# Decoder trunk on one core: in 24 of 80 groups of products the columns are walked in another order

## The chip, the cores and the metric

The kernel runs on one core of one Trainium2 chip. The metric is the device time in microseconds (us) of one execution; the median of three runs is quoted. A profile of one execution, taken by the hardware, gives the rows that are read below. TensorE is called PE in them, its loading of stationary operands PEld, VectorE DVE, ScalarE ACT, GpSimd POOL and SyncE SP.

## The reference

The program is a decoder trunk of two layers over 256 tokens with 2048 features, all in float32. Cut to what matters:

```python
for layer in range(2):
    h = rms_norm(x, norm_g[layer])
    proj = h @ w_in[layer]                                  # 256 x 2048 by 2048 x 14336
    q, k, v, g_att, glu_a, glu_b, g_conv = split(proj)      # 2048 columns each
    q, k = apply_rope(rms_norm(q)), apply_rope(rms_norm(k))
    att = dilated_mixture(q, k, v)                          # 16 heads of 128
    att_y = rms_norm(att, att_out_g[layer]) * silu(g_att)
    u = depthwise_conv31(glu_a * sigmoid(glu_b)) + dw_bias
    conv = silu(layer_norm(u)) @ w_pw[layer]                # 2048 x 2048
    conv_y = rms_norm(conv, conv_out_g[layer]) * silu(g_conv)
    x = x + concat(att_y, conv_y) @ w_out[layer]            # 4096 x 2048
```

## The kernel before

**The large products.** All weights are cut into groups: a group is 2048 rows by 512 columns of one matrix, and its result is 256 tokens by 512 columns, in two banks of PSUM, `ps[0]` and `ps[1]`, of 128 tokens by 512 columns each. A layer has 40 groups: for each quarter `j` of the features `glu_b`, `glu_a`, `v`, `q`, `k` (20 groups); then `g_conv` 0, `g_att` 0 to 3, `g_conv` 1 to 3; then four `o_att`, four `pw` and four `o_conv`. So there are 80 groups in two layers, and `g_att`, `g_conv` and `o_att` have eight each.

**Steps.** A group is eight steps. A step has one weight tile of two times 128 rows by 512 columns (512 KB), loaded by SP's queue into `raw` (L220). ScalarE rounds it to the float32r tile `whi` (L227), VectorE writes the remainder to `wlo` (L228). The stationary operand, 128 features by 128 tokens, has such a pair too, `sthi` and `stlo`. TensorE makes three products for each 128 rows and each half of the tokens:

```python
T.matmul(ps[tt], xh, hi[:, kk], start=(k == 0), stop=False)
T.matmul(ps[tt], xh, lo[:, kk], start=False, stop=False)
T.matmul(ps[tt], xl, hi[:, kk], start=False, stop=(k == KT - 1))
```

These are L629, L630 and L631: 12 in a step, 96 in a group, 7680 in all. In each the moving operand is 512 columns of float32r, read from SBUF in the order in which they lie, and the 512 sums are written and added to in the same order in one bank. Splits are put into the program three steps ahead.

**The rest of the work.** Everything else (rotary positions, attention, the depthwise convolution, norms, transposes) is made of tasks that are cut into slices. The class `Filler` puts a slice into the program behind a step where its estimate of each engine's progress says that it fits. It estimates a step at 2.6 us of TensorE. The order of every engine's instructions is thus fixed when the program is built.

**Who uses the sums.** When a group is done, a task empties its banks: `ev_g_att` (ScalarE, L507), `ev_g_conv` (ScalarE, L501), `ev_o_att` (VectorE, L517). There are four banks for the sums, so the next group fills two while the former two are emptied. These tasks read 512 columns in the order in which they lie.

Of the kernel before, what the change touches and what calls it, by code (L numbers as in the profile page):

```python
# [22 lines left out]
KT = D // 128  # L23
NCH = 4
CH = 512
EPS = 1e-6
# Columns of the per-feature parameters: the taps by layer, then pairs by layer.
P_BIAS, P_LNG, P_LNB, P_ATT, P_CONV = (DEPTH * CW + DEPTH * i for i in range(5))
NPRM = DEPTH * (CW + 5)

# Weight tiles of [128, KS, CH]: a step is the products of one of them.
KS = 2
NSTEP = KT // KS
R_RAW, R_SPLIT = 4, 4
AHEAD = 3


class Need:
    """What the next slice of a task takes: time by engine (us, in the order in which its operations follow
    from one another), PSUM banks, and a condition that has to hold first."""  # L40

    def __init__(self, banks=0, when=None, **time):
        self.banks, self.when, self.time = banks, when, list(time.items())
# [3 lines left out]


class Filler:
    """Work beside the large products, in slices between their steps.  # L50

    A task is a generator that yields the Need of its next slice. The engines work in program order, so a
    slice is put into the program where its operands will about have been computed, by an estimate of how
    far each engine has got, and not where it would make the splits of the next weight tiles late."""

    HOP = 0.2

# [29 lines left out]
            self.banks.append((b, self.now[4]))  # L87

    def use(self, time, ready):
        """The time at which operations that follow from one another end, the first not before ready."""  # L90
        start = end = ready
        for e, cost in time:
            start = max(self.t[e], start)
            end = max(start + cost, end + 0.3)
            self.t[e] = end
            if e == "G":  # shares VectorE's port
                self.t["V"] = max(self.t["V"], start) + cost
                end += 1.0
            start += 0.45
        return end + self.HOP  # L100
# [43 lines left out]
def trunk(ctx: ExitStack, tc: tile.TileContext, x, norm_g, w_in, q_norm_g, k_norm_g, dw_kernel, dw_bias,  # L144
# [6 lines left out]
    V, S, G, T = nc.vector, nc.scalar, nc.gpsimd, nc.tensor  # L151

    def t(shape, name, dt=F32):
        return sb.tile(shape, dt, name=name)

    # Stationary operands by chunk of four contraction tiles, as exact sums hi + lo of float32r.
    st_hi = [[t([128, 4, SEQ], f"sthi{s}{c}", F32R) for c in range(4)] for s in range(2)]
    st_lo = [[t([128, 4, SEQ], f"stlo{s}{c}", F32R) for c in range(4)] for s in range(2)]
    Y = [t([128, 4 * SEQ], f"y{c}") for c in range(4)]
    A = [t([128, 2, CH], f"a{c}") for c in range(4)]  # L160
# [35 lines left out]

    xs = [dr.tile([SEQ, CH], F32, name=f"xs{c}") for c in range(NCH)]

# [1 line left out]
    groups = []  # L200
    for l in range(DEPTH):
        for j in range(NCH):
# [7 lines left out]
    tiles = [(g, s) for g in range(len(groups)) for s in range(NSTEP)]  # L210
# [12 lines left out]
    def split(i):  # L223
        if i >= len(tiles):
            return
        a, hi = raw[i % R_RAW], whi[i % R_SPLIT]
        S.activation(hi, a, AF.Copy)  # L227
        V.tensor_sub(wlo[i % R_SPLIT], a, hi.bitcast(F32))  # L228
        halved[i] = fill.use([("A", 0.95), ("V", 1.14)], loaded[i])
        load(i + R_RAW)  # L230

# [1 line left out]
    ready = [[False] * 4 for _ in range(2)]  # a chunk of the operand is in place  # L233
    vacant = [[True] * 4 for _ in range(2)]  # all its products are in the program
    flags = set()

    def flag(*what):
# [2 lines left out]
    def has(*what):  # L240
        return lambda: what in flags

    def rsqrt(r, ss, scale, n):
        """r = (ss * scale + EPS) ** -0.5 on [128, n]"""
        G.tensor_scalar(r, ss, scale, EPS, op0=ALU.mult, op1=ALU.add)
        G.tensor_tensor(r, r, half[:, :n], op=ALU.pow)

    def transposes(src, banks):
        """[128 tokens, 2, 4 x 128] -> two banks of [128, 2, 256 tokens]"""
        for b in range(2):  # L250
            for i in range(2):
                for tt in range(2):
                    e = (2 * b + i) * 128
                    T.transpose(banks[b][:, i * SEQ + tt * 128:i * SEQ + tt * 128 + 128],  # L254
                                src[:, tt, e:e + 128], ident)

    def to_stationary(src, s, c, gain):
        """Transposes a chunk and splits it, times a gain per feature."""
        yield Need(2, lambda: vacant[s][c], P=0.9)
        banks = [fill.bank(), fill.bank()]  # L260
        transposes(src, banks)
        yield Need(A=1.5, V=1.6)
        p = [b[:, i * SEQ:(i + 1) * SEQ] for b in banks for i in range(2)]
        for i in range(4):
            S.activation(st_hi[s][c][:, i], p[i], AF.Copy, scale=gain(i))  # L265
        for i in range(4):
            V.scalar_tensor_tensor(st_lo[s][c][:, i], p[i], gain(i), st_hi[s][c][:, i].bitcast(F32),  # L267
                                   op0=ALU.mult, op1=ALU.subtract)
        fill.free(*banks)
        filled(s, c)  # L270

    def filled(s, c):
        vacant[s][c] = False
        ready[s][c] = True

    def x_chunk(l, c):
        """A chunk of the residual stream, in A, becomes the next layer's operand."""
        yield from to_stationary(A[c], 0, c, lambda i: ng[:, l * KT + 4 * c + i:l * KT + 4 * c + i + 1])
        fill.add(x_square(l, c), 3, fill.now[4])

    def x_square(l, c):
        yield Need(A=1.4)
        for tt in range(2):
            S.activation(junk, A[c][:, tt], AF.Square, accum_out=ssx[:, tt, c:c + 1])  # L284
        flag("x", l, c)
        if all(("x", l, k) in flags for k in range(4)):
            yield Need(V=0.1, G=0.6)
            V.tensor_reduce(rsc, ssx, axis=mybir.AxisListType.X, op=ALU.add)
            rsqrt(rx, rsc, 1.0 / D, 2)
            flag("rx", l)  # L290
# [58 lines left out]
    def ln_square(l, j):  # L349
# [23 lines left out]
        V.tensor_copy(rsc, ps[:, 0:4:2])  # L373
        fill.free(ps)
        rsqrt(rstd, rsc, 1.0 / D, 2)
        G.tensor_copy(rbc, rstd[:, :, None].to_broadcast([128, 2, 128]))
        yield Need(1, P=0.5)
# [165 lines left out]
            yield from x_chunk(l + 1, j)  # L543
            nc.sync.dma_start(xs[j].rearrange("(t p) e -> p t e", p=128), A[j])

# [1 line left out]
    ng_in = t2[:DEPTH * KT, :128]  # L547
    S.dma_start(ng_in, norm_g.rearrange("l (k p) -> (l k) p", p=128))
    make_identity(nc, ident)
# [6 lines left out]
    r = 0  # L556
# [45 lines left out]
    for c in range(NCH):  # L602
        fill.add(x_chunk(0, c), 0)
    fill.add(parameters(), 1, 45.0)
    split(0)

# [1 line left out]
    users = {"glu_b": ev_glu_b, "glu_a": ev_glu_a, "v": ev_v, "g_conv": ev_g_conv, "g_att": ev_g_att,  # L608
             "pw": ev_pw, "o_att": ev_o_att, "o_conv": ev_o_conv,
             "q": lambda l, j, ps: ev_qk(l, j, ps, "q"), "k": lambda l, j, ps: ev_qk(l, j, ps, "k")}  # L610
# [1 line left out]
    for i, (g, s) in enumerate(tiles):  # L612
        l, nm, j, _, _, _, st = groups[g]
        c = s * KS // 4
        fill.until(lambda: ready[st][c])
        if s == 0 and g >= 2:
            fill.until(has("ev", *groups[g - 2][:3]))
        for a in range(i + AHEAD if i else 1, i + AHEAD + 1):
            split(a)
        ps = [acc[(2 * g + tt) % 4] for tt in range(2)]  # L620
        hi, lo = whi[i % R_SPLIT], wlo[i % R_SPLIT]
        order = [(kk, tt) for kk in range(KS) for tt in range(2)]
        if s == NSTEP - 1:
            order.sort(key=lambda o: o[1])
        for kk, tt in order:
            k = s * KS + kk
            tok = slice(tt * 128, tt * 128 + 128)
            xh, xl = st_hi[st][c][:, k % 4, tok], st_lo[st][c][:, k % 4, tok]
            T.matmul(ps[tt], xh, hi[:, kk], start=(k == 0), stop=False)  # L629
            T.matmul(ps[tt], xh, lo[:, kk], start=False, stop=False)  # L630
            T.matmul(ps[tt], xl, hi[:, kk], start=False, stop=(k == KT - 1))  # L631
        fill.use([("P", 2.6)], halved[i])
        if i >= 2 and later:
            nc.sync.dma_start(*later.pop(0))
        if i == NSTEP:
            G.dma_start(mask, log_count)
            rope_tables(0)
        if s % 2 and j == NCH - 1 and nm in last[st]:
            ready[st][c], vacant[st][c] = False, True
        if s == NSTEP - 1:  # L640
            fill.add(users[nm](l, j, ps), 0, fill.t["P"])
            if nm == "o_att" and j == NCH - 1 and l + 1 < DEPTH:
                rope_tables(l + 1)
        fill.run()
# [8 lines left out]


def log_counts():
    """By query (in its tile of 128) and key: the log of how many branches attend it."""
    q = np.arange(SEQ)[:, None]
    k = np.arange(SEQ)[None, :]
    d = q - k
    count = np.zeros((SEQ, SEQ))  # L660
    for window, dil in ((128, 1), (512, 4), (2048, 16)):
        count += (d >= 0) & (d <= window) & (d % dil == 0)
    m = np.where(count > 0, np.log(np.maximum(count, 1)), -1e30).astype(np.float32)
    return np.ascontiguousarray(np.concatenate([m[:128, :128], m[128:]], 1))
# [23 lines left out]
```

## Time and profile before

| what | value |
|---|---|
| median of three runs | 1864.1 us |
| the three runs | 1864.1, 1865.67 and 1863.65 us |
| span of the profiled execution, first to last instruction | 1863.1 us |
| TensorE busy | 1849.6 us, 99% |
| VectorE busy | 1394.8 us, 75% |
| ScalarE busy | 988.8 us, 53% |
| moved by DMA | 349.98 MB, 188 GB/s over the span |

The page gives no time for the profiled execution other than its span; the runs' median lies 1.0 us above that. The duration of a matmul in the rows is from its start to its modelled end; consecutive ones overlap, so what one takes of the span is read from the distance between two starts, or from a count in a stretch. A large product has one record; a float32 product of the small kind (L451, L452 and the like) has two records for one instruction of the program, so that a row of 64 stands for 32 of them.

### The profile page before, as it was taken

How to read it: one execution, taken by the hardware profiler on the slowest of the kernel's cores; microseconds unless marked ns; L12 is line 12 of the kernel's file. 1: busy time of each engine (PE TensorE's matmuls, PEld its weight loads, DVE VectorE, ACT ScalarE, POOL GpSimd, SP SyncE). 2: the span in 40 equal slices, each digit the busy share in tenths (PEclk: the TensorE clock that was granted, in tenths of full speed). 3: DMA queues.
4: the chain of work that ended last, by engine and by line, in shares of the span. 5: the costliest groups of instructions: out<-in, count | busy, mean ns of one | idle time of the engine just before them, and what ended most of it. 6: DMA issues, size and time to landing. Idle time of an engine off the chain costs nothing.

```text
span 1863.1 us, 23820 instructions
## 1 busy us (share of the span) xinstructions
PE 1849.6 (99%) x8525; PEld 1541.2 (83%) x8525; DVE 1394.8 (75%) x2160; ACT 988.8 (53%) x1559; POOL 136.3 (7%) x153
## 2 busy tenths in 40 slices
PE   8999999999999999999999999999999999999999
PEld 6888888888888888888888888888888888888887
DVE  4778889888889885556558888797887998755554
ACT  5465564564654464445444655646556445644542
POOL 1110100100110140000000101002000102100000
PEclk9999999999999999999999999999999999999999
DMA  7765656656566676666666656566565666666564
GB/s 237 204 184 167 180 180 180 182 168 190 174 180 193 177 231 210 192 190 190 208 203 192 188 161 184 159 199 183 160 185 165 194 195 190 213 204 195 178 205 145
DMA packets 180880, 349.98 MB, mean 188 GB/s; under 512 B 11064, under 2 KB 11096, under 8 KB 180760
## 3 DMA queue, kind: packets, MB, share of 16 engines
q1 hardware_dynamic: 179176, 345.61, 61.2%
q0 software_dynamic: 960, 1.77, 0.5%
q8 instruction: 67, 1.10, 0.2%
q10 hardware_dynamic: 624, 1.07, 0.2%
q14 instruction: 53, 0.43, 0.1%
HBM read 344.21 MB, written 4.19 MB: 187 GB/s over the span
## 4 chain that ended last, share of the span: by engine, by line
PE 97%; DMA 2%; ACT 0%; SPq 0%; DVE 0%; issue 0%; ACTq 0%; DVEq 0%
PE acc L630 31%; PE acc L631 31%; PE acc L629 31%; PE ax L254 2%; DMA raw<-in_w_in 2%; PE ax L452 1%; PE ax L469 1%; PE ax L478 0%; PE ax L477 0%; PE ax L476 0%; PE ax L451 0%; ACT whi L227 0%; DVE wlo L228 0%; SPq L551 0%; ACT junk L284 0%
## 5 line engine op out<-in xcount | busy, mean ns | idle before, releaser
L228 DVE TENSOR_TENSOR wlo<-raw,whi 128x1024 fp32r<-128x1024 f32 x640 | 792.2, 1246 | 404.5 <-ACT whi L227 400.4
L227 ACT ACTIVATE whi<-raw 128x1024 fp32r<-128x1024 f32 x640 | 675.3, 1063 | 671.1 <-PE acc L631 471.5
L629 PE MATMUL acc<-whi,sthi 128*128 128x512 f32 x2560 | 1005.9, 393 | 2.7 <-ACT whi L227 2.7
L630 PE MATMUL acc<-wlo,sthi 128*128 128x512 f32 x2560 | 998.1, 390 | 0.8 <-DVE wlo L228 0.8
L631 PE MATMUL acc<-whi,stlo 128*128 128x512 f32 x2560 | 998.3, 390 | 0.0
L629 PEld LDWEIGHTS acc<-whi,sthi 128*128 128x128 f32 x2560 | 481.7, 188 | 100.9 <-ACT whi L227 3.1
L631 PEld LDWEIGHTS acc<-whi,stlo 128*128 128x128 f32 x2560 | 481.5, 188 | 101.0
L630 PEld LDWEIGHTS acc<-wlo,sthi 128*128 128x128 f32 x2560 | 481.8, 188 | 98.8 <-DVE wlo L228 1.1
L326 DVE SCALAR_TENSOR_TENSOR y<-ut,prm,y 128x256 f32<-128x256 f32 x960 | 411.1, 486 | 0.0
L414 POOL TENSOR_SCALAR qr<-qss 128x8 f32<-128x8 f32 x16 | 3.2, 197 | 692.1 <-ACT junk L411 692.1
L411 ACT ACTIVATE junk<-acc,rx 128x128 bf16<-128x128 f32 x128 | 47.1, 368 | 8.4 <-PE acc L631 4.8
L334 POOL TENSOR_TENSOR ysum<-ysum,y 128x256 f32<-128x256 f32 x30 | 31.8, 1058 | 237.1 <-DVE y L326 235.7
L421 ACT ACTIVATE d<-acc,qr 128x128 f32<-128x128 f32 x128 | 34.8, 383 | 18.0 <-POOL qr L416 18.0
L265 ACT ACTIVATE sthi<-ax,prm 128x256 fp32r<-128x256 f32 x64 | 25.1, 475 | 31.1 <-PE ax L254 31.1
L267 DVE SCALAR_TENSOR_TENSOR stlo<-ax,prm,sthi 128x256 fp32r<-128x256 f32 x64 | 26.5, 475 | 15.8 <-ACT sthi L265 15.8
L442 ACT ACTIVATE c<-ax 128x512 f32<-128x512 f32 x32 | 17.4, 597 | 33.6 <-PE ax L254 33.6
L465 ACT ACTIVATE sm<-sm,smm 128x128 f32<-128x128 f32 x64 | 28.2, 443 | 6.6 <-DVE smm L460 6.6
L362 POOL TENSOR_TENSOR ssum<-ssum,d 128x512 f32<-128x512 f32 x14 | 26.8, 1912 | 5.9 <-ACT d L355 5.0
L415 POOL TENSOR_TENSOR qr<-qr,half 128x8 f32<-128x8 f32 x16 | 26.3, 1642 | 1.3
L254 PEld LDWEIGHTS ax<-ident,d 128*128 128x128 f32 x192 | 22.4, 140 | 3.2
L254 PE MATMUL ax<-ident,d 128*128 128x128 f32 x192 | 24.9, 273 | 0.0
L411 ACT ACTIVATION_READ_ACCUMULATOR junk<-acc,rx 128x1 f32 x128 | 24.7, 193 | 0.0
(106 smaller groups left out, 669.4 us busy)
## 6 DMA issues: line engine op xcount, KB each, us to landing
raw<-in_w_in SPq DMA_DIRECT2D x448, 512.0 KB, 3.9
raw<-in_w_out SPq DMA_DIRECT2D x128, 512.0 KB, 4.6
raw<-in_w_pw SPq DMA_DIRECT2D x64, 512.0 KB, 4.6
a<-in_x SPq DMA_DIRECT2D x8, 512.0 KB, 5.7
xs<-a SPq DMA_DIRECT2D x4, 512.0 KB, 6.0
a<-xs SPq DMA_DIRECT2D x4, 512.0 KB, 6.5
out<-a SPq DMA_DIRECT2D x4, 256.0 KB
out<-a ACTq DMA_DIRECT2D x4, 256.0 KB, 5.1
```

Of the source, the lines that this page charges most:

```text
L227: S.activation(hi, a, AF.Copy)
L228: V.tensor_sub(wlo[i % R_SPLIT], a, hi.bitcast(F32))
L254: T.transpose(banks[b][:, i * SEQ + tt * 128:i * SEQ + tt * 128 + 128], src[:, tt, e:e + 128], ident)
L326: V.scalar_tensor_tensor(y[:, c], u[:, c, k:k + SEQ], w[:, c, l * CW + k:l * CW + k + 1], y[:, c], op0=ALU.mult, op1=ALU.add)
L334: G.tensor_add(ysum, ysum, y[:, c])
L362: G.tensor_add(ssum, ssum, half_sq)
L411: S.activation(junk[:, :DH], ps[tt][:, h * DH:(h + 1) * DH], AF.Square, scale=rx[:, tt:tt + 1], accum_out=qss[:, tt, h:h + 1])
L421: S.activation(n[:, tt, h * DH:(h + 1) * DH], ps[tt][:, h * DH:(h + 1) * DH], AF.Copy, scale=qr[:, tt, h:h + 1])
L465: S.activation(s[:, cs], s[:, cs], AF.Exp, bias=m[:, tt:tt + 1], scale=-1.0, accum_out=lsum[:, tt:tt + 1])
L629: T.matmul(ps[tt], xh, hi[:, kk], start=(k == 0), stop=False)
L630: T.matmul(ps[tt], xh, lo[:, kk], start=False, stop=False)
L631: T.matmul(ps[tt], xl, hi[:, kk], start=False, stop=(k == KT - 1))
```

## The change

In the groups of three names the moving operand and the sums are seen through a rearranged view. The 512 columns are taken as 2 or 4 equal parts; a run of 4, 32 or 16 columns is taken from the first part, then one from the next, and so on until all parts are through, then the next run of each. The view is the same for both operands, so each column's sum lands where it did before. The stationary operand, the number and order of instructions, the loads, the splits and the tasks that read the sums are as before. The lines of comment that the diff also removes change nothing in the program.

| groups | count | parts | run (columns, bytes) | distance between parts | runs in one product |
|---|---|---|---|---|---|
| `g_att` | 8 | 2 | 4, 16 | 256 columns | 128 |
| `g_conv` | 8 | 2 | 32, 128 | 256 columns | 16 |
| `o_att` | 8 | 4 | 16, 64 | 128 columns | 32 |

```diff
+WALK = {"g_att": (2, 4), "g_conv": (2, 32), "o_att": (4, 16)}
+
+
+def walk(nm, v):
+
+    if nm not in WALK:
+        return v
+    parts, run = WALK[nm]
+    return v.rearrange("p (a b e) -> p b a e", a=parts, e=run)
...
-            T.matmul(ps[tt], xh, hi[:, kk], start=(k == 0), stop=False)
-            T.matmul(ps[tt], xh, lo[:, kk], start=False, stop=False)
-            T.matmul(ps[tt], xl, hi[:, kk], start=False, stop=(k == KT - 1))
+            o, h, lw = (walk(nm, v) for v in (ps[tt], hi[:, kk], lo[:, kk]))
+            T.matmul(o, xh, h, start=(k == 0), stop=False)
+            T.matmul(o, xh, lw, start=False, stop=False)
+            T.matmul(o, xl, h, start=False, stop=(k == KT - 1))
```

## Rows read from the trace of the kernel before

**Rows 1.** The view of the cores: span and mean granted clock.

```profile
core 0: 1863.1 us, clock 0.998
```

**Rows 2.** The page's part 1: busy time of each engine.

```profile
PE 1849.6 (99%) x8525; PEld 1541.2 (83%) x8525; DVE 1394.8 (75%) x2160; ACT 988.8 (53%) x1559; POOL 136.3 (7%) x153
```

**Rows 3.** The page's part 4: shares of the chain that ended last.

```profile
PE 97%; DMA 2%; ACT 0%; SPq 0%; DVE 0%; issue 0%; ACTq 0%; DVEq 0%
PE acc L630 31%; PE acc L631 31%; PE acc L629 31%; PE ax L254 2%; DMA raw<-in_w_in 2%; PE ax L452 1%; PE ax L469 1%; PE ax L478 0%; PE ax L477 0%; PE ax L476 0%; PE ax L451 0%; ACT whi L227 0%; DVE wlo L228 0%; SPq L551 0%; ACT junk L284 0%
```

**Rows 4.** The waits of TensorE over the whole span.

```profile
engine line waited for: us in total, times, longest us
PE ax L594 <- DMA t<-in_norm_g: 3.9, 1, 3.9
PE acc L629 <- ACT whi L227: 2.7, 1, 2.7
PE ax L254 <- DMA a<-in_x: 1.8, 2, 1.1
PE acc L630 <- DVE wlo L228: 0.8, 1, 0.8
```

**Rows 5.** Windows, L629 alone: g_att 1 to 3, g_conv 1, o_att 1 to 3, pw 0 to 2.

```profile
core 0: us, PE busy (x) PEld busy (x), PEclk, DMA share, GB/s
536.90:602.20 65.30, 37.34 (x96) 18.02 (x96) 1.00 0.67 194
602.20:623.90 21.70, 12.45 (x32) 6.01 (x32) 1.00 0.67 193
694.70:759.90 65.20, 37.34 (x96) 18.00 (x96) 1.00 0.66 209
759.90:825.20 65.30, 37.34 (x96) 18.02 (x96) 1.00 0.61 193
```

**Rows 6.** Timeline of TensorE: first and last product of group g_att 1.

```profile
537.15 0.39 PE L629 MATMUL acc<-whi,sthi 128*128 128x512 f32 x1
...
558.68 0.39 PE L631 MATMUL acc<-whi,stlo 128*128 128x512 f32 x1
```

**Rows 7.** Timeline of TensorE: small float32 products in the group before g_att 0.

```profile
506.80 0.60 PE L452 MATMUL ax<-c,c 128*128 128x256 f32 x2
507.24 0.38 PE L451 MATMUL ax<-c,c 128*128 128x128 f32 x2
507.46 0.60 PE L452 MATMUL ax<-c,c 128*128 128x256 f32 x2
507.89 0.38 PE L451 MATMUL ax<-c,c 128*128 128x128 f32 x2
```

**Rows 8.** One line's instructions (ns, least, median, most): L309, L442.

```profile
L309 ACT ACTIVATE ut<-ax x16: 592/597/598, 67.3 to 1343.5; 128x512 f32<-128x512 f32 x16
L442 ACT ACTIVATE c<-ax x32: 594/598/600, 125.6 to 1424.2; 128x512 f32<-128x512 f32 x32
```

**Rows 9.** Groups by form, whole span: those that empty the walked sums.

```profile
L517 DVE SCALAR_TENSOR_TENSOR a<-acc,ra,a 128x512 f32<-128x512 f32 x16 | 11.2, 744 | 0.0
L507 ACT ACTIVATE d<-acc,rx 128x512 f32<-128x512 f32 x16 | 11.1, 693 | 7.7 <-PE acc L631 7.7
L501 ACT ACTIVATE c<-acc,rx 128x512 f32<-128x512 f32 x16 | 10.7, 697 | 3.9 <-PE acc L631 3.9
```

**Rows 10.** Windows, all engines: g_att 1 to 3, o_att 1 to 3.

```profile
core 0: us, PE busy (x) PEld busy (x) DVE busy (x) ACT busy (x) POOL busy (x), PEclk, DMA share, GB/s
536.90:602.20 65.30, 65.30 (x289) 54.05 (x288) 59.82 (x100) 29.33 (x30) 0.00 (x0) 1.00 0.67 194
694.70:759.90 65.20, 65.20 (x289) 54.01 (x288) 38.74 (x35) 32.24 (x36) 3.83 (x6) 1.00 0.66 209
```

**Rows 11.** Groups by form, whole span: the three lines of the large products.

```profile
L629 PE MATMUL acc<-whi,sthi 128*128 128x512 f32 x2560 | 1005.9, 393 | 2.7 <-ACT whi L227 2.7
L631 PE MATMUL acc<-whi,stlo 128*128 128x512 f32 x2560 | 998.3, 390 | 0.0
L630 PE MATMUL acc<-wlo,sthi 128*128 128x512 f32 x2560 | 998.1, 390 | 0.8 <-DVE wlo L228 0.8
```

## The prediction

> **What bounds the kernel now.** I read the view of the cores first, for the clock: the mean granted clock is 0.998, so TensorE runs at the upper of its two levels, 2.4 GHz, nearly throughout [rows 1]. Then the busy times: TensorE 99%, with VectorE next at 75% [rows 2]. A busy TensorE may still be one that waits inside its instructions, so the chain that ended last comes third: 97% of it is TensorE, 93% the three lines of the large products [rows 3]. The waits of TensorE come fourth: four kinds, 9.2 us in all, and they lie in the start, where the first operands come in [rows 4]. In a stage of large products there is none.
>
> So the kernel is a stream of products, and its price is the distance between two starts. Two views give that. In the windows, 96 instructions of L629, thus 288 products, fill 65.30 us in `g_att` 1 to 3: 226.7 ns each; the windows of `g_conv` and `o_att` give 226.0 and 226.4 ns, and `pw`, which the change leaves alone, 226.7 [rows 5]. In the timeline, the 96 starts of group `g_att` 1 go from 537.15 to 558.68, 95 distances of 226.6 ns [rows 6]. The modelled duration of 390 ns [rows 11] is no price; it contains the overlap with the next product. I take 226.7 ns for 512 columns, or 0.443 ns for a column. The reader is to see how even this is: it does not vary with what the DMAs or VectorE do, so nothing but TensorE's own stream sets it.
>
> **What the change touches.** 24 groups of 96 products are 2304 products, 2304 x 226.7 ns = 522 us, 28% of the span. All of that stands on the chain. There is no cover for it: a nanosecond more on each of these products costs 2.3 us at the end, and one less gives it back, as long as the other engines keep up.
>
> Nothing is added or removed in number. The same 2304 products are issued in the same order with the same stationary operands. Loads, splits, tasks and their places in the program stay: the planner's costs are constants and know nothing of the walk. SP's queue and POOL's are not passed by anything. Because both views are rearranged alike, each sum lies where it lay, and the instructions that empty the banks read them in the old way, at 693, 697 and 744 ns [rows 9]: no term there. If the rearranged views made the program take semaphores otherwise, the waits would be on tiles that were split long ago; waits already met cost nothing that can be seen in the stage, so this term is 0 too, and the work that hides it is the splits' lead of three steps.
>
> What is left is one unknown: whether a product whose columns come in runs takes longer than 226.7 ns. The trace has no broken walk on TensorE, so I bound it by the nearest rows.
>
> - Above: the slowest stream of columns that TensorE shows here. The small float32 products of L452 stream 256 columns twice in 507.24 - 506.80 = 0.44 and 507.89 - 507.46 = 0.43 us, so 217 ns for 256 columns, 0.85 ns a column: half the rate of the large products [rows 7]. At that rate a product of 512 columns takes 434 ns, 207 more. For all 2304 that is +477 us.
> - Below: the same rows say that a stream which is no faster per pass than 217 ns for 256 columns at half rate would be 217 ns for 512 at full rate. The large products stand 10 ns above that. Should those 10 ns hang on the order of columns, a new order could lose them: 2304 x 10 ns = -23 us. VectorE could follow: it is busy 59.82 of 65.30 us in `g_att` [rows 10], and the stretch would shrink by 288 x 10 ns to 62.4.
> - Between: ScalarE writes 512 columns in 597 ns in two runs of 256 with a gap between them (L309, into the padded `ut`), and 598 ns without a gap (L442) [rows 8]. One break in 512 columns costs that engine nothing that can be seen. It is another engine and one break, not 127, but it is the nearest row in kind.
>
> I take 0 for the unknown. The reason is how the runs compare with the plain walk: in all three settings a run holds at least four columns next to one another, 16 bytes, and starts at a multiple of its length, so any reading or writing in aligned pieces of two or four columns takes as many pieces as before. Only the addresses of the pieces jump. The mechanism that would charge for that must look at more than four columns at a time, or must charge for the jump itself; nothing in the rows speaks for either, and the row in kind speaks against the second. The sum is then 1863.1 us of span, +0 for 768 products in runs of 4, +0 for 768 in runs of 32, +0 for 768 in runs of 16, and 1.0 us that lies around the span in the median of the runs: 1864.1, which I give as 1864.
>
> The Trainium skill has a rule that speaks against the change. Its page "PSUM — Partial Sum Buffer", section "Specifications (TRN2)", says of PSUM's 8-byte lines that any pattern which isn't contiguous slows matmuls significantly. By that sentence alone the three kinds of groups would all pay, whatever their runs. The page "Advanced Engine Details and Errata", section "Memory Cachelines", repeats it and then narrows it: every two consecutive elements should be contiguous, and in SBUF two hits on a 16-byte line are enough. By that one all three walks would be free, as runs of 4 satisfy both. No row here shows which holds; the sum goes by the bounds above.
>
> **The rivals.**
>
> 1. Each jump costs TensorE the time of one column. Place: all walked products. Jumps in a product: 127, 15 and 31. Price: 768 x (127 + 15 + 31) x 0.443 ns = 58.9 us, of which 43.2 in `g_att`, 5.1 in `g_conv`, 10.5 in `o_att`. It gives 1923. For it: 0.443 ns is all that a column has, so a stream that must turn an inner loop of four columns has little time for it. Against: the one break of L309 [rows 8]. It decides from 3.7 us on, which is 0.028 ns a jump. This is the rival on the other side.
> 2. Runs of 4 alone fall to half rate, because more than 16 bytes are fetched or written at once, and runs of 64 and 128 bytes do not. Place: `g_att`. Price: 768 x 207 ns = 159 us, so 2023. For it: TensorE does have a half rate [rows 7], and 16 bytes is the shortest run here. Against: the large and the small products read four bytes a column alike, and I see no sign in the rows of a wider piece.
> 3. Any broken walk falls to half rate: +477 us, 2341. This is how the first of the two sentences of the skill would look here, priced by rows. Against: ScalarE's rows, and that the runs keep neighbours together.
> 4. The 10 ns above the full rate go: -23 us, 1841. For it: the surplus is there and I can't name its cause [rows 5, 7]. Against: it is the same in every group at every time, so it looks like a fixed charge for each product, which an order of columns doesn't touch.
>
> That the views don't reach the instruction as written, for instance because equal rearrangements of both operands are undone, would give the forecast's time as well and is no case of its own.
>
> **How the numbers follow.** No change: 0.70. Rival 1, or any small price for a jump: 0.11. Rival 2: 0.08. Rival 3: 0.06. Rival 4: 0.05. The time is that of the first, 1864. What a measurement of this kernel can tell from no change is about 0.2%, 3.7 us: so faster 0.05, same 0.70, slower 0.11 + 0.08 + 0.06 = 0.25. The runs before spread over 2.0 us, so the first case alone lies within 1860 to 1868. To leave out no more than 2 in 10, the range reaches up to the first rival, whose bound is 1923: 1859 to 1925 holds 0.81. Rivals 2 and 3 above and 4 below are left out with 0.19.
>
> **What the profile after would show.** If I am right: the windows over each of the three stages have 288 products in 65.3 us as before, L629 to L631 keep one duration near 390 ns in all groups, and no new wait of TensorE appears. Each rival has its own mark. Under rival 1 the three stages differ by their jumps: distances of 283 ns in `g_att`, 233 in `g_conv`, 240 in `o_att`, and 226.7 elsewhere. Under rival 2 `g_att` alone stands at 434 ns. Under rival 3 all three stand there. Under rival 4 the three are at 217 and `pw` is not. In every slower case ScalarE and VectorE wait longer for TensorE and nothing else becomes late, since each split would have more time. The prediction is wrong if TensorE charges for a jump of address, or takes more than four columns at a time, in SBUF or in PSUM: the trace of before can't exclude either, and because the stages have no cover, the whole charge would be seen in the time.

## The result and the profile after

The changed kernel takes 1893.49 us against 1864.35 us: a ratio of 1.0156, 95% interval 1.0144 to 1.0168. The forecast of no change was wrong; the time lies in the range, between the forecast and the first rival.

The stream of products is where the time went. The first view is that of the cores, the second the windows over whole groups, with L642 (L629 before) alone; the windows run from the first start of `g_att` 1, `g_conv` 1, `o_att` 1 and `pw` 1 to that of the next group, so each holds 96 products.

```profile
core 0: 1891.7 us, clock 0.998
```

```profile
core 0: us, PE busy (x) PEld busy (x), PEclk, DMA share, GB/s
540.16:564.16 24.00, 13.30 (x32) 6.05 (x32) 1.00 0.62 175
612.16:634.88 22.72, 12.78 (x32) 6.05 (x32) 1.00 0.62 184
707.86:730.05 22.19, 12.39 (x32) 6.08 (x32) 1.00 0.78 234
796.21:817.97 21.76, 12.45 (x32) 6.01 (x32) 1.00 0.62 195
```

The clock is the one of before, 0.998 [rows 1]. Divided by 96 the stretches are 250.0, 236.7, 231.1 and 226.7 ns for a product, where all four stood at 226 to 227 [rows 5]. So `g_att` pays 23.3 ns, `g_conv` 10.0 and `o_att` 4.4, while `pw`, which isn't walked, pays nothing. Over 768 products each that is 17.9 + 7.7 + 3.4 = 29.0 us; the spans differ by 1891.7 - 1863.1 = 28.6, so the account is closed to 0.4 us. (Distances between starts below are such means over the products of one group, most without its first or last step. A whole stretch over 96 differs from them by 1.3 ns at most, but for one: 8 parts by runs of 8 take 236.4 over the whole group and 233.5 behind the first step.)

The timeline of TensorE shows that the price is paid inside the stream, from the first start of `g_att` 1 to the last:

```profile
540.16 0.41 PE L642 MATMUL acc<-whi,sthi 128*128 128x512 f32 x1
540.41 0.42 PE L643 MATMUL acc<-wlo,sthi 128*128 128x512 f32 x1
...
563.91 0.42 PE L644 MATMUL acc<-whi,stlo 128*128 128x512 f32 x1
```

The 95 distances fill 23.75 us, 250 ns on average (246 and 254 in turn), where they were 226.6 [rows 6]. The waits of TensorE are the four of before, within 0.1 us each [rows 4]:

```profile
engine line waited for: us in total, times, longest us
PE ax L606 <- DMA t<-in_norm_g: 4.0, 1, 4.0
PE acc L642 <- ACT whi L239: 2.7, 1, 2.7
PE ax L266 <- DMA a<-in_x: 1.7, 2, 1.0
PE acc L643 <- DVE wlo L240: 0.7, 1, 0.7
```

### The profile page after: what moved, and what is told of

Its sections match the earlier page's. It is cut to its first block, busy times and chain, and to the rows that moved or that the text cites. A ratio compares the mean times of both kernels' runs of the same rounds, so it can differ in the third digit from the quotient of the medians.

```text
span 1891.7 us, 23820 instructions
## 1 busy us (share of the span) xinstructions
PE 1878.1 (99%) x8525; PEld 1543.3 (82%) x8525; DVE 1392.9 (74%) x2160; ACT 990.8 (52%) x1559; POOL 137.8 (7%) x153
## 4 chain that ended last, share of the span: by engine, by line
PE 97%; DMA 1%; ACT 1%; SPq 0%; issue 0%; DVE 0%; ACTq 0%
PE acc L643 31%; PE acc L644 31%; PE acc L642 31%; PE ax L266 2%; DMA raw<-in_w_in 1%; PE ax L464 1%; PE ax L481 1%; PE ax L489 0%; PE ax L490 0%; PE ax L488 0%; PE ax L463 0%; ACT whi L239 0%; ACT sthi L277 0%; ACT junk L296 0%; DVE wlo L240 0%
## 5 line engine op out<-in xcount | busy, mean ns | idle before, releaser
L642 PE MATMUL acc<-whi,sthi 128*128 128x512 f32 x2560 | 1014.9, 396 | 2.7 <-ACT whi L239 2.7
L643 PE MATMUL acc<-wlo,sthi 128*128 128x512 f32 x2560 | 1009.0, 394 | 0.7 <-DVE wlo L240 0.7
L644 PE MATMUL acc<-whi,stlo 128*128 128x512 f32 x2560 | 1009.3, 394 | 0.0
L642 PEld LDWEIGHTS acc<-whi,sthi 128*128 128x128 f32 x2560 | 482.9, 189 | 109.8 <-ACT whi L239 3.1
L643 PEld LDWEIGHTS acc<-wlo,sthi 128*128 128x128 f32 x2560 | 482.3, 188 | 108.0 <-DVE wlo L240 1.1
```

The costliest lines, as they stand in the source:

```text
L642: T.matmul(o, xh, h, start=(k == 0), stop=False)
L643: T.matmul(o, xh, lw, start=False, stop=False)
L644: T.matmul(o, xl, h, start=False, stop=(k == KT - 1))
```

## The experiments

**Which side pays.** The first run walks the moving operand alone, the second the sums alone, in the same 24 groups.

```diff
+WALK = {"g_att": (2, 4, "m"), "g_conv": (2, 32, "m"), "o_att": (4, 16, "m")}
...
-            o, h, lw = (walk(nm, v) for v in (ps[tt], hi[:, kk], lo[:, kk]))
+            o = walk((l, nm, j), ps[tt], "s")
+            h, lw = (walk((l, nm, j), v, "m") for v in (hi[:, kk], lo[:, kk]))
```

That is the first run; the second has `"s"` in place of `"m"` in the first line. `walk` leaves a view as it is when its side isn't named there.

> Only the moving operand (the weight tiles in SBUF) is walked, in the same 24 groups and by the same runs; the sums are written plainly, so columns of these groups land in another order than the reference's. Theory R (the reading side pays): all of the 29 us come back, near 1893 us, with distances between starts of 250 ns in g_att, 237 in g_conv, 231 in o_att, as in the changed kernel. Theory W (the writing side, the sums in PSUM, pays): 1864 us, 226.7 ns in all groups. If each side pays a part: in between, and the two parts add up to 29 us over this run and the next.

> Only the sums are walked, in the same 24 groups; the moving operand is read plainly, so columns of these groups land in another order than the reference's. Theory W: 1893 us and 250, 237 and 231 ns. Theory R: 1864 us, 226.7 ns throughout.

The moving operand alone: 1893.84 us, ratio 1.0156 (1.0141 to 1.0171). The sums alone: 1864.83 us, ratio 1.0001 (0.9991 to 1.0010). Theory R (the reading pays) holds and theory W (the writing pays) falls. The windows over `g_att` 1 to 3, `g_conv` 1 and `o_att` 1 to 3 (L643 alone), first with the moving operand walked, then with the sums walked:

```profile
540.10:612.10 72.00, 39.89 (x96) 18.14 (x97) 1.00 0.60 175
612.10:634.80 22.70, 12.78 (x32) 6.01 (x33) 1.00 0.64 184
707.80:774.40 66.60, 37.20 (x96) 18.28 (x97) 1.00 0.65 204
```

```profile
536.90:602.20 65.30, 37.36 (x97) 18.02 (x96) 1.00 0.68 196
602.20:623.90 21.70, 12.39 (x33) 6.01 (x32) 1.00 0.66 195
694.70:759.90 65.20, 37.26 (x97) 18.02 (x96) 1.00 0.67 210
```

In the first the 288 products of `g_att` take 72.0 us, as in the changed kernel; in the second 65.3, as before [rows 5]. The reading of the weight tiles from SBUF pays all of it, and the writing of the sums nothing.

**Which walks pay.** As the price shows in the distances between starts, one run can try a setting in each of 31 groups without small products. This run and the others of this kind below were executed once, and each setting is read from the 96 products of one group.

```diff
+WALK = {
+    (0, 'q', 0): (2, 2, "sm"),
+    (0, 'q', 1): (2, 4, "sm"),
...
+}
```

> Both sides are walked, each of 31 groups that hold no small products by a setting of its own (2 to 128 parts, runs of 2 to 128); all other groups are plain. Theory J (a price for each jump, whatever its distance): at one length of run the number of parts doesn't matter, and the price falls with the run: 23 ns more at 4, then 6 at 16 and 3 at 32. Theory D (the distance of the parts or their number decides, as the changed kernel's 10 ns for 15 jumps over 256 columns and 4.4 ns for 31 jumps over 128 columns suggest): at runs of 16 two parts cost more than four, and at runs of 32 four parts cost less than the 10 ns of two. By a rule of lines of two columns, runs of 2 cost no more than runs of 4.

Distances between starts in ns, by parts and length of run in columns:

| parts | run 2 | 4 | 8 | 16 | 32 | 64 | 128 |
|---|---|---|---|---|---|---|---|
| 2 | 340.0 | 250.0 | 243.3 | 240.0 | 236.7 | 226.7 | 226.7 |
| 4 | 443.3 | 267.9 | 231.1 | 231.1 | 233.3 | 226.7 | 226.7 |
| 8 | 486.7 | 278.2 | 233.5 | 239.6 | 236.7 | 226.7 | |
| 16 | 453.3 | 246.7 | 230.6 | 240.0 | 226.7 | | |
| 32 | 431.1 | 223.3 | 232.3 | | | | |
| 64 | 461.4 | 231.1 | | | | | |
| 128 | 451.1 | | | | | | |

Four of its rows (windows over one group each, L675 alone: 2 parts by 2, 2 by 4, 8 by 4, 32 by 4):

```profile
86.94:119.56 32.62, 16.40 (x32) 6.33 (x32) 1.00 0.47 133
216.08:240.09 24.01, 13.29 (x32) 6.05 (x32) 1.00 0.61 178
847.31:874.00 26.69, 14.31 (x33) 6.14 (x32) 1.00 0.50 161
1535.15:1556.62 21.47, 12.30 (x33) 5.99 (x32) 1.00 0.66 188
```

Theory J falls: at runs of 4, with 127 jumps each time, a product takes from 278 down to 223 ns, and the last is less than plain. Theory D (the distance or the number of the parts decides) holds at 16 (240.0 from two parts, 231.1 from four) and at 32 (236.7 and 233.3). The settings of the change have the prices that they had there, though two of them stand in other groups here (2 by 4 in one of `q`, 2 by 32 in one of `g_att`), so a price belongs to the setting and not to the stage. Runs of 2 cost 340 to 487 ns, so the last sentence of the expectation missed. Runs of 64 cost nothing from two, four or eight parts.

**Is it the stationary operand?** TensorE loads the next one while it reads the moving one (PEld is busy 83% of the span beside PE's 99% [rows 2]), so the two might get in each other's way.

```diff
...
+    v = tile[:, k % 4, tt * 128:tt * 128 + 128]
+    if how == "b1":
+        return v[:, 0:1].to_broadcast([128, 128])
+    if how[:1] == "m":
+        return v[:, :int(how[1:])]
+    if how[:1] == "s":
+        n = int(how[1:])
+        return tile.rearrange("p k t -> p (k t)")[:, 512 * tt * (n < 8):512 * tt * (n < 8) + 128 * n:n]
...
+            xh, xl = (still(key, z[st][c], k, tt) for z in (st_hi, st_lo))
```

> 31 groups, each with a walk of the moving operand and the sums, and a stationary operand changed in what is read for it: one column read 128 times (b1), 128 columns at a step of 2, 4 or 8 (s2, s4, s8), or only the first 96, 64 or 32 columns (m96, m64, m32; the rest of the tokens get no products). Those groups compute something else than the reference. Theory L (the loading of the next stationary operand and the reading of the moving one get in each other's way, and a broken walk makes it worse): a plain product falls from 227 towards 213 to 217 ns with b1, about half the way with m64, and rises with s8; the walks by 4 from 2, 4 and 8 parts, 250, 268 and 278 ns, fall to about 216 with b1. Theory S (the moving operand's own reading is what stalls): the stationary operand doesn't matter, 227, 250, 268 and 278 ns stay as they are under b1, s2, s8 and m64.

Plain products: 231.1 ns with one column read 128 times, 230.0 with 96 or 64 columns, 231.7 with 32; 233.3, 235.0 and 244.5 at steps of 2, 4 and 8. Walks by 4 from two, four and eight parts, with one column: 248.8, 266.6 and 277.0. Five of the windows, each over one group (L693 alone): plain with one column, with a step of 8 and with 64 columns; then the walks from two and from four parts with one column.

```profile
85.05:107.24 22.19, 12.70 (x32) 6.01 (x32) 1.00 0.66 192
441.67:465.13 23.46, 12.99 (x32) 10.49 (x33) 1.00 0.63 183
561.04:583.12 22.08, 12.60 (x33) 4.28 (x32) 1.00 0.66 192
605.36:629.24 23.88, 13.21 (x32) 6.06 (x32) 1.00 0.61 178
725.57:752.13 26.56, 14.16 (x32) 6.14 (x32) 1.00 0.49 158
```

Theory L (the loading of the stationary operand gets in the way) falls as the cause: the walks keep their price when one column is read again and again for the stationary operand, and a plain product doesn't get shorter. Theory S (the moving operand's own reading stalls) holds for these walks, but not to the nanosecond, and the two do meet: a step of 8 adds 18 ns to a plain product, 2 to the walk by 4 from two parts (252.2), and 23 to that from 32 parts (246.1 against 223.3).

**All groups with the one setting that was shorter than plain.**

```diff
+WALK = {}
...
+def walk(key, v, side):
+    return v.rearrange("p (a b e) -> p b a e", a=32, e=4)
...
```

> All 80 groups are walked, both sides, from 32 parts by runs of 4, the one setting of the sweep that was shorter than plain (223.6 ns against 226.7); the sums land as in the reference. If the gain is a property of the setting: 7680 x 3.1 ns = 24 us less than before, 1841 us. If it belonged to that one group (its weight tiles, its neighbours): within 2 us of before, 1864.

It takes 1856.87 us, ratio 0.9955 (0.9938 to 0.9971) to the kernel before: 8.0 us less, a third of what was expected. Three of its windows, each over one group (`q` 0 and `g_att` 1 of the first layer, `o_conv` 1 of the second; L640 alone):

```profile
87.10:108.54 21.44, 12.29 (x32) 5.99 (x32) 1.00 0.67 195
534.60:556.37 21.77, 12.38 (x33) 6.00 (x32) 1.00 0.67 200
1786.45:1807.89 21.44, 12.29 (x32) 5.99 (x32) 1.00 0.70 222
```

The same setting runs at 223.3 ns in some groups and at 226.8 in others; of 32 groups without small products 4 have the lower value. They give 1.3 us of the gain; the rest comes from groups with small products, in parts of which the lower value stands too. The single distances say more: at the lower value they repeat every four products (221, 218, 230 and 224 ns), at the upper every seven. Of 36 unbroken stretches of 48 and more large products (one with a wait in it is left out), 13 stand at the lower value and 23 at the upper, each from its ninth product to its end, over all borders of groups. So the value changes only where small products break the stream, and a product's time depends on those before it. What picks the value behind such a break stays open.

**Distance or loop?** The moving operand is read by patterns of its own from the 1024 columns of its tile.

```diff
...
+    n, d, r, off = WALK[key]
+    f = tile.rearrange("p k c -> p (k c)")
...
+    if n == 1:
+        return f[:, None, off:off + 4].to_broadcast([128, 128, 4])
+    f = f[:, off:off + n * d].rearrange("p (a c) -> p a c", a=n)
+    if r == 0:
+        return f[:, None, :, 0:4].to_broadcast([128, 128 // n, n, 4])
+    return f[:, :, 0:512 // n].rearrange("p a (b e) -> p b a e", e=r)
...
```

> The sums are plain; in 31 groups the moving operand is read by an access pattern of its own out of the 1024 columns of its weight tile, so these groups compute something else than the reference. Seventeen settings read only one, two, four or eight places of four columns, again and again, at distances of 4 to 512 columns; thirteen walk by runs of 4 at distances that are no power of two (260 to 320 columns from two parts, 132 to 160 from four, 68 and 80 from eight, 36 and 48 from sixteen, 20 from thirty-two); one reads plainly from column 2. Theory B (places whose addresses stand at certain distances can't be read one right after the other, as in a memory of several banks): the time depends on the distance alone, two places read in turn cost more at some distances than at others, and the walks lose their price at some distance near the old one: 2 parts at 260 to 320 columns fall from 250 towards 227 or below, 8 parts at 68 or 80 from 278. Theory A (the loop of the access pattern itself costs, at each step of its outer loops): the distance doesn't matter, 250 ns for all walks from two parts, 268 from four, 278 from eight, 247 from sixteen, 224 from thirty-two. Read from column 2, where a run of four no longer begins at a multiple of 16 bytes: under both 227, as all columns are still neighbours.

Theory A (the loop costs, whatever the distance) falls. Four parts by runs of 4 at 128 columns cost 267.9 ns in the sweep; at 144 columns the same loops cost 226.7. Eight parts at 64 columns cost 278.2, at 80 columns 224.4. Two parts fall less: 251.1 at 260 columns, 240.0 at 272 and 288, and 250.0 again at 320. One place or two places of four columns, read again and again, cost 216.5 to 216.8 ns at every distance tried. Four places cost 286.7 at a distance of 64 or 256 columns, 228.9 at 16 and 241.8 at 4. So two places at 256 columns are free, while the walk of `g_att`, two parts at 256 columns, pays 23.3 ns: the distance of two neighbours in turn isn't the whole price. The walk from 32 parts shows it too: at 20 columns it costs 270.7, where the sweep had 223.3 at 16. The windows over one group each (L685 alone): one place; four places at 16; four at 64; the walk from four parts at 144; from eight at 80.

```profile
88.53:109.32 20.79, 12.20 (x33) 6.03 (x32) 1.00 0.65 193
...
733.03:755.11 22.08, 12.41 (x32) 6.05 (x32) 1.00 0.59 189
755.11:782.63 27.52, 14.48 (x32) 6.19 (x32) 1.00 0.49 156
...
1644.42:1666.17 21.75, 12.44 (x32) 6.02 (x32) 1.00 0.45 150
1710.42:1731.97 21.55, 12.42 (x32) 5.98 (x32) 1.00 0.62 195
```

Read plainly from column 2 a product costs 233.3, not the 227 expected under both: this start, 8 bytes behind a multiple of 16, costs 6.6 ns.

**The sums alone, by shorter runs.** Seventeen groups have a setting with the side `"s"` alone.

> Only the sums are walked, in 17 groups, by runs of 2, 4, 8 and 16 from 2 to 128 parts; their columns land in another order than the reference's. If the sums are free at any pattern of pairs: 226.7 ns in all. If there is a limit that the three settings of the changed kernel didn't reach: runs of 2 are slower than runs of 4.

All 17 settings, runs of 2 from 2 to 128 parts among them, stand at 226.7 ns. The window of one (2 parts by runs of 2; L661 alone):

```profile
87.32:109.08 21.76, 12.45 (x33) 6.01 (x32) 1.00 0.65 192
```

The sums are free at any pattern of pairs that was tried; single columns were not tried.

**More distances.** The code of the probe, with 31 other settings.

> The sums are plain; in 31 groups the moving operand is read in a walk of its own (parts, distance in columns, run), so these groups compute something else than the reference. Theory B, sharpened after the probe: only the distance modulo 64 columns (256 bytes) counts. So from two parts 384 columns give 250 ns like 256 and 320, and 336 and 304 near 240; from four parts 192 gives 268 like 128, and 208 gives 227 like 144; from eight parts 72 to 112 all stay under 245, far from the 278 at 64, and 124 and 68, each 4 off a multiple, are alike (230); the best pitch from eight or sixteen parts is below 222. Theory A (the loop costs, whatever the distance) is out if 192 and 208 differ. If the modulus is another one, 384 from two parts or 192 from four parts shows it.

Two parts at 384 columns cost 250.0, at 416 240.0, as at 288; four parts at 192 cost 267.9 and at 208 226.7, as at 128 and 144. There the modulus of 64 columns holds; two parts at 336 cost 242.2 and at 272 240.0, so it isn't exact for all walks. Eight parts at 88 columns cost 280.0, at 124 237.8 against 230.1 at 68, and no pitch came below 224.4: three misses. The dearest walk by 4 is that from 32 parts at 24 columns, 313.3. With eight parts and more, more goes on than the distance of neighbours tells. Four of the windows (L685 alone): eight parts at 88; four at 192 and at 208; two at 384.

```profile
442.61:469.49 26.88, 14.31 (x32) 6.27 (x32) 1.00 0.54 158
...
1486.53:1512.26 25.73, 13.97 (x33) 6.24 (x32) 1.00 0.58 171
1512.26:1534.03 21.77, 12.46 (x33) 6.02 (x32) 1.00 0.67 190
1698.02:1722.03 24.01, 13.29 (x32) 6.05 (x32) 1.00 0.53 175
```

**The change with runs of 64.**

```diff
+WALK = {"g_att": (2, 64, "sm"), "g_conv": (2, 64, "sm"), "o_att": (2, 64, "sm")}
```

> The change with another setting: the same 24 groups, both sides, from two parts by runs of 64 columns; the sums land as in the reference. The sweep had 226.7 ns for it: 1864 us, no change to before, though TensorE still walks 2304 products with 7 jumps in each. If the walk as such cost something that the sweep's single group hid, it would be above 1868.

1863.94 us, ratio 0.9998 (0.9989 to 1.0008). Seven jumps in each of 2304 products cost nothing that can be seen.

**A map of distances.** Four places of four columns in turn, the code of the probe.

> The sums are plain; in 31 groups a product reads only four places of four columns, again and again, at one distance (8 to 240 columns), so these groups compute something else than the reference. It measures the price of a distance by itself. Theory B (the distance modulo 64 columns counts): 128 and 192 give 287 ns like 64 and 256 in the probe, 80, 144 and 208 all give the 229 ns of 16, and pairs such as 24, 88 and 32, 96, 160 are alike. If 24 is dear by itself, it explains the 280 ns that the walk from eight parts at 88 columns had against the expectation; if 24 and 88 are cheap here, that price has another cause, and stays open.

With the values of the probe, in ns by the distance in columns:

| distance mod 64 | distances and ns |
|---|---|
| 0 | 64: 286.7, 128: 286.7, 192: 286.7, 256: 286.7 |
| 4 | 4: 241.8, 68: 241.9 |
| 8 | 8: 242.2, 72: 242.2 |
| 12 | 12: 236.7, 76: 236.7 |
| 16 | 16: 228.9, 80: 228.9, 144: 228.9, 208: 228.9 |
| 24 | 24: 260.0, 88: 260.0 |
| 32 | 32: 254.4, 96: 254.4, 160: 254.4, 224: 254.4 |
| 40 | 40: 243.3, 104: 243.3 |
| 48 | 48: 237.8, 112: 237.8, 176: 237.8, 240: 237.8 |
| 56 | 56: 249.3, 120: 249.3 |
| 60 | 60: 246.7, 124: 246.7 |
| others | 20: 226.7, 28: 256.7, 36: 243.3, 44: 246.7, 52: 243.3 |

Six of its rows (windows over one group each, L685 alone: 24, 80, 88, 128, 144 and 192 columns):

```profile
445.17:470.00 24.83, 13.54 (x32) 6.11 (x32) 1.00 0.59 171
1153.98:1175.96 21.98, 12.36 (x32) 6.05 (x32) 1.00 0.66 193
1272.48:1297.32 24.84, 13.54 (x33) 6.11 (x32) 1.00 0.57 170
1656.62:1684.14 27.52, 14.52 (x32) 6.27 (x32) 1.00 0.46 152
1684.14:1706.10 21.96, 12.35 (x33) 6.05 (x32) 1.00 0.59 190
1753.33:1780.85 27.52, 14.48 (x33) 6.19 (x32) 1.00 0.47 153
```

The modulus holds for all eleven residues that were read at two distances or more, to 0.1 ns. 24 is the dearest after 0, which fits the 280.0 ns of eight parts at 88. But four parts by runs of 4 at 152 columns, also 24 modulo 64, cost only 230.0 in the run before. So the map doesn't give the price of a walk.

**The price in all groups.**

> All 80 groups are walked, both sides, from two parts by runs of 4 (the setting of g_att); the sums land as in the reference. The suspected price in all 7680 products instead of 768: if nothing covers it anywhere, 7680 x 23.3 ns = 179 us more than before, 2043 us. If other stages have cover, less.

One run: 2036.46 us, 172 more than the 1864.21 of the kernel before beside it, and 7 less than expected. In groups without small products the distance is 250 ns throughout; a group with 24 small products (`glu_a` 3) grew by 26.75 - 24.61 = 2.14 us where 96 x 23.3 ns would be 2.24. So nearly all groups have no cover.

One group has, and it makes up most of the 7 us: `glu_a` 0 of the first layer took 26.27 us, where the kernel before takes 29.45 and the price would add 2.24. In the kernel before TensorE waits there 2.7 us for `whi` [rows 4], and 13 products behind that wait start 427 ns apart, at the lower granted clock of 1.2 GHz. With all groups walked, the products ahead of it are slower, so `whi` is no longer late: the wait is gone, and so are the 427 ns. First the whole group and that stretch in the kernel before (all engines), then the group with all groups walked:

```profile
core 0: us, PE busy (x) PEld busy (x) DVE busy (x) ACT busy (x) POOL busy (x), PEclk, DMA share, GB/s
34.34:63.79 29.45, 26.04 (x109) 20.70 (x108) 12.80 (x12) 12.23 (x13) 9.54 (x17) 0.88 0.76 214
47.17:52.71 5.54, 5.54 (x14) 4.28 (x13) 3.64 (x3) 3.14 (x3) 2.52 (x4) 0.50 0.90 246
```

```profile
36.53:62.80 26.27, 25.49 (x110) 18.67 (x108) 12.36 (x12) 11.83 (x13) 7.68 (x13) 1.00 0.75 221
```

## Why the prediction was wrong

**What bounds the kernel** was right: the stream of products, at 226.7 ns each, and no cover in the walked groups. Each nanosecond came through to the end: 29.0 us by the products, 28.6 in the span. That no stage of large products has a wait was not quite so: those for `whi` and `wlo` [rows 4] lie in `glu_a` 0, which the change doesn't walk.

**No term elsewhere** was right too: the waits of TensorE stayed, and with the sums walked alone the time was that of before.

**The unknown taken as 0** is the step that failed: the cost of a jump of address in a walked product. In its place the runs showed 23.3, 10.0 and 4.4 ns a product, 29.0 us in all, paid by the reading of the moving operand alone. The reason for the 0 was that runs of at least four columns let any aligned reading take as many pieces as before, and that only the addresses of the pieces jump. That runs of at least four columns are cheaper held: runs of 2, which halve a piece of 16 bytes, cost 340 to 487 ns. But where the next piece lies matters as well, and that was set aside because nothing in the rows spoke for it. Nothing in them could speak against it either: the row in kind was another engine with one break, between two runs of 256 columns [rows 8], and runs of 64 and more are free on TensorE as well. I read a row as evidence on 127 breaks that could only be evidence on one.

**The 10 ns above the full rate** [rows 5, 7], which the prediction took for a fixed charge of a product, aren't fixed: a product that reads one place again and again takes 216.5 ns, with its sums written plainly and the stationary operand as before. So they hang on the reading of the moving operand too, and an order of the same 512 columns that is cheaper than the plain one was found (223.3 ns).

**Rival 1** named the right engine and sign, and the wrong measure. It priced a jump at one column: 43.2, 5.1 and 10.5 us for the three stages, against 17.9, 7.7 and 3.4. It has `o_att` with its 31 jumps above `g_conv` with 15, and the trace has them the other way round. Rivals 2 and 3 fell: no stage is near 434 ns. Rival 4 fell as put, as no walk of the change lost the 10 ns. That the time lies in the range is luck in part: its upper end is the price of rival 1, whose measure was wrong.

The rule of the Trainium skill that was weighed, that any pattern which isn't contiguous slows matmuls (page "PSUM — Partial Sum Buffer", section "Specifications (TRN2)"), gave the sign and not the place: the price is in SBUF's reading, and 19 settings of the sums alone, the three of the change among them, left a product at 226.7 ns. The narrower form of the Trainium skill, on the page "Advanced Engine Details and Errata", section "Memory Cachelines", asks for pairs in PSUM, which agrees, and for two hits on a 16-byte line of SBUF, which doesn't: runs of 2 are two such hits, and cost 340 ns and more; runs of 4 are four, and cost up to 278. The measurements decide.

**What is shown, and what stays open.** Shown: the whole price of the change lies in reading the moving operand. At a given number of parts it changes with the distance between them, and distances that are equal modulo 64 columns, or 256 bytes, had the same price, to 0.1 ns in the map and to 2.2 ns in the walks from two and four parts. It doesn't follow the number of jumps, the loops of the pattern or the sums, and with one column read for the stationary operand the walks by 4 from two, four and eight parts took 1.2 or 1.3 ns less, no more. Not shown is the mechanism. A memory whose parts serve one place at a time, by address modulo 256 bytes, would fit the four places; that two places at 256 columns are free speaks against its simplest form. Open is also why 24 columns are so much dearer than 16 or 20 in the map (260.0 against 228.9 and 226.7) and hardly in a walk from four parts, why eight parts differ from four, and what picks the level of the walk from 32 parts.

## What to carry to other kernels

Where TensorE's stream of products has no cover, the order in which a product reads its moving operand is a cost of its own: keep runs of 64 float32r columns or more; with shorter ones, don't put four or more places that are read in turn at multiples of 256 bytes from one another, and measure the distance, as no rule found here gives the price of a walk beforehand. The sums may be walked by pairs at no cost, so a permutation is better put on that side. Where the trace has no row of an operation, a row of another engine with a fraction of its breaks is no bound; the chance has to stay wide, and one run with a setting in each of many groups gives the whole table.

## What the runs showed of the hardware that was not expected

- A plain float32r product of 512 columns takes 226.7 ns, and 216.5 if it reads one place of four columns again and again: 10 ns of each plain product, 7680 x 10.2 ns = 78 us of this kernel, hang on which places of SBUF are read, and in which order. The best order of all 512 columns that was tried takes 223.3 ns, and only behind some breaks of the stream.
- Four places at a multiple of 256 bytes from one another cost 286.7 ns for 512 columns, at 64 bytes 228.9; two places took 216.8 at most at any distance tried, and a walk from two parts 240.0 at least with runs of 4.
- Reading from a start 8 bytes behind a multiple of 16 cost 6.6 ns a product, and the stationary operand at a step of 8 columns 18 ns in a plain one.
- The time of a product can depend on those before it: the walk from 32 parts by runs of 4 stays at 223.3 or at 226.7 ns from one break of the stream to the next.
